# A fixed order for the first weight blocks, two small banks for the first values, and a last norm factor formed earlier

## The chip, the cores and the metric

The kernel runs on one NeuronCore of a Trainium2 chip. TensorE (PE in the profile; PEld are its weight loads) multiplies, VectorE (DVE), ScalarE (ACT) and GpSimd (POOL) work on rows, and SyncE (SP) issues nearly all transfers. The metric is the device time of one execution in microseconds (us), lower is better; a kernel is judged by the median of its runs. A profiled execution is a run of its own: its span is the time between the first and the last record on the core, and its own time is a little longer than that.

## The reference, cut to what matters

Two layers work on 256 positions of 2048 features. Layer 0 mixes with HGRN2, a gated recurrence with 16 heads; layer 1 mixes with a gated MLP. Each layer then has a squared-ReLU MLP, and a last norm closes the trunk.

```python
def rms_norm(x, gain):
    y = xf * lax.rsqrt(jnp.mean(xf * xf, axis=-1, keepdims=True) + NORM_EPS)
    return (y * gain.astype(jnp.float32)).astype(x.dtype)

def hgrn2_mixer(h, w_in, w_out, g_norm, lb):
    proj = h @ w_in                                   # (256, 2048) @ (2048, 8192)
    q, f, i, g = jnp.split(proj, [FORGET_DIM, 2 * FORGET_DIM, 2 * FORGET_DIM + D_MODEL], axis=-1)
    q = jax.nn.silu(q)
    forget = lb + (1.0 - lb) * jax.nn.sigmoid(f)
    k = 1.0 - forget
    log_f = jnp.log(forget)
    v = i
    ...                                               # decayed scores of q and k, times v, chunk by chunk
    return o @ w_out

for i in range(DEPTH):
    hn = rms_norm(h, norm_mix[i])
    h = h + mixer(hn)
    h = h + sq_relu_mlp(rms_norm(h, norm_mlp[i]), mlp_w1[i], mlp_w2[i])
return rms_norm(h, final_norm)
```

## The kernel before, in words

All large products are done in two parts. ACT casts each block of weights to a rounded high part (line 128), DVE subtracts that from the block and leaves the low part (line 129), and PE forms high x high and low, then low x high, in PSUM (lines 159 and 161 where features come out on partitions, 170 to 172 where positions do). The activations `S1` hold a high and a low half in the same way. Each weight tile (`wt`) holds 1024 numbers of 128 rows in both parts; there are five such buffers, and three raw buffers (`raw`) that SP loads ahead.

HGRN works on pairs of heads, `hp` from 0 to 7. The weight blocks are used in the order forget gate, query, values, output gate; the values of two pairs are formed together (every even `hp`), 512 columns wide, by `mm_wide` in `pw2`. For the first pair the forget block (`pw0`, `pw_149` in the order of instructions) and the query block (`pw1`, `pw_150`) are special: x arrives in four chunks of 512 features, and for each chunk `to_features` transposes it on PE (line 196), scales it by the norm's gain into the high and low half of `S1` (line 200 on ACT, 201 on DVE), and both weight blocks are multiplied for the chunk. The squares of x (lines 260 and 263) are summed beside that, and only when all are there is the norm's factor `r0c` formed: a mean on DVE (lines 265 to 268), a power on POOL (line 269), a spread over all partitions by two matmuls on PE (`pb_a`, line 276), a copy into `R0`. The products of `pw0` and `pw1` are taken out of PSUM (lines 179, 180), multiplied by `R0` (line 182), and a long chain on ACT and DVE follows (lines 326 to 413): exponentials, logarithms, a running sum `c` (line 340), differences `dl` and decayed factors `gl`. From these PE forms the scores (`sc` line 420, `sd` line 428, `st` line 435, `sx` line 440), which DVE copies under masks into `Px` and `Pm`.

PSUM is split into two pools: two wide tiles of two banks each (`psw`, tag `pw`) and four single banks (`pss`, which hands out a bank for every transpose, score and spread by `bank(name)`). `pw2`, the first values, takes a wide tile, and so waits until `pw0` has been taken out.

Which instruction stands where in each engine's queue is decided while the program is built, by a scheduler with a timeline of its own; the code's order and `tc.high_priority` are only hints to it. Every engine then runs its queue in the order that it was given.

At the end the last 512 columns are done in two blocks of 256, for 128 positions at a time. `last_rows` adds the product to the stream, squares it with a running sum on ACT (line 644), and multiplies it by the last gain on DVE (line 645); `finish` forms the row factor (lines 669 to 671), scales four pieces of 512 columns on DVE and ACT in turn (lines 675, 677) and sends them out (line 678).

Of the kernel before, what the change touches and what calls it, by code (L numbers as in the profile page):

```python
# [8 lines left out]
F32 = mybir.dt.float32  # L9
# [6 lines left out]
P = 128  # L16
# [17 lines left out]
def trunk(ctx: ExitStack, tc: tile.TileContext, x, norm_mix, norm_mlp, final_norm, hgrn_w_in, hgrn_w_out,  # L34
# [83 lines left out]

    def split_weights(n, raw, q, parts=1):
# [3 lines left out]
        wt = pool.tile([P, 2048], FR, tag=tag, name=f"wt{n}_{q}").rearrange("p (k n) -> p k n", k=kw)  # L123
        src = raw[:, kw * (q % 2):kw * (q % 2) + kw, :]
        with tc.high_priority(offset=PRIO if n > 1 else 0):
            for i in range(parts):
# [3 lines left out]
        ready.setdefault(n, []).append(wt)  # L130

# [24 lines left out]
    def mm_feat(pt, wts, xs, ks=range(KT), run=8):  # L156
        for tiles in runs(wts, xs, ks, run):
            for wt, xk, k, n in tiles:
                M.matmul(pt[:, n, :], lhsT=wt[:, n * P:(n + 1) * P], rhs=xk, start=(k == 0), stop=False)  # L159
            for wt, xk, k, n in tiles:  # L160
                M.matmul(pt[:, n, 256:512], lhsT=wt[:, 256 + n * P:256 + (n + 1) * P], rhs=xk[:, 0:256],  # L161
                         start=False, stop=(k == KT - 1))

    def mm_wide(pt, wts, xs):
        for k in range(KT):
            wt = wts[k // 2][:, k % 2, :]
            xk = xs[k // 2][:, k % 2, :]
            for n in range(2):
                hi, lo = xk[:, n * P:(n + 1) * P], xk[:, 256 + n * P:256 + (n + 1) * P]
                M.matmul(pt[:, n, :], lhsT=hi, rhs=wt[:, 0:512], start=(k == 0), stop=False)  # L170
                M.matmul(pt[:, n, :], lhsT=hi, rhs=wt[:, 512:1024], start=False, stop=False)  # L171
                M.matmul(pt[:, n, :], lhsT=lo, rhs=wt[:, 0:512], start=False, stop=(k == KT - 1))  # L172

# [14 lines left out]

    def to_features(c, gains):

        for i in (2 * c, 2 * c + 1):
            pt = bank(f"xT{i}")
            for k in range(2):
                o = (2 * i + k) * P
                for j in range(2):
                    M.transpose(pt[:, k * T + j * P:k * T + (j + 1) * P], ht[:, j, o:o + P], ident)  # L196
            for k in range(2):
                g = gains[:, 2 * i + k:2 * i + k + 1]
                ptk = pt[:, k * T:(k + 1) * T]
                S.activation(S1[i][:, k, 0:256], ptk, AF.Copy, scale=g)  # L200
                V.scalar_tensor_tensor(S1[i][:, k, 256:512], ptk, g, f32(S1[i][:, k, 0:256]),  # L201
                                       op0=ALU.mult, op1=ALU.subtract)
# [7 lines left out]
    cols = cp.tile([P, 81], F32, name="cols")  # L210
    if WARM:
        wps = bank("wps")
        for i in range(WARM):
            M.matmul(wps[:, 0:P], lhsT=ones, rhs=ones, start=True, stop=True)
    warm = cp.tile([P, 1], F32, name="warm")
    S.activation(warm, epsc, AF.Exp)
# [4 lines left out]
    with tc.tile_pool(name="x0", bufs=1) as x0, tc.tile_pool(name="x1", bufs=2) as x1:  # L221
# [15 lines left out]
        pw = [psw.tile([P, 2, 512], F32, tag="pw", name=f"pw{n}") for n in range(2)]  # L237
        pc = bank("pc0")
        M.transpose(pc[:, 0:32], rows0, ident[0:32, 0:32])
        V.tensor_copy(cols0, pc[:, 0:32])  # L240
# [14 lines left out]
        V.tensor_copy(cols, pc[:, 0:81])  # L255
        for c in range(4):
            for j in range(2):
                junk = x1.tile([P, 512], F32, tag="junk", name=f"junk{c}{j}")
                if j:
                    V.scalar_tensor_tensor(junk, xt[c][:, j, :], 1.0, xt[c][:, j, :], op0=ALU.mult, op1=ALU.mult,  # L260
                                           accum_out=ssp[:, j, c:c + 1])
                else:
                    S.activation(junk, xt[c][:, j, :], AF.Square, accum_out=ssp[:, j, c:c + 1])
        s2 = x0.tile([P, 2, 2], F32, name="s2")
# [34 lines left out]
    with tc.tile_pool(name="hg", bufs=1) as hg, tc.tile_pool(name="hg2", bufs=2) as hg2:  # L299
# [14 lines left out]
        for hp in range(NP):  # L314
# [129 lines left out]
            if hp % 2 == 0:  # L444
                wts, pt = take()
                mm_wide(pt, wts, S1)
                vv = hg.tile([P, 2, 512], F32, tag="v", name=f"v{hp}")
                for j in range(2):
                    with tc.high_priority(offset=PRIO_EV):
                        S.activation(vv[:, j, :], pt[:, j, :], AF.Copy, scale=r0c[:, j:j + 1])  # L450
            v = vv[:, :, hp % 2 * 256:hp % 2 * 256 + 256]
# [189 lines left out]

    def normed(hs, c0, width, i, j):
        jk = fin2.tile([P, 512], F32, tag="jk", name=f"jk{i}{j}")
        S.activation(jk[:, 0:width], hs, AF.Square, accum_out=ssf[:, j, i:i + 1])
        V.tensor_tensor(hs, hs, fnb[:, c0:c0 + width], op=ALU.mult)

# [7 lines left out]
    def last_rows(pj, wts, i, j):  # L654
# [10 lines left out]
        V.scalar_tensor_tensor(hs, pj, r2c[:, j:j + 1], hs, op0=ALU.mult, op1=ALU.add)  # L665
        normed(hs, c0, 256, i, j)

    def finish(j):
        V.tensor_tensor(mf[:, j:j + 1], ssf[:, j, 4:5], pre[:, j:j + 1], op=ALU.add)
        V.tensor_scalar(mf[:, j:j + 1], mf[:, j:j + 1], 1.0 / D, EPS, op0=ALU.mult, op1=ALU.add)  # L670
        G.tensor_tensor(rf[:, j:j + 1], mf[:, j:j + 1], mhalf[:, 0:1], op=ALU.pow)
        for c, w in enumerate((512, 512, 512, 512)):
            hs = ht[:, j, c * 512:(c + 1) * 512]
# [4 lines left out]
            (nc.sync, nc.scalar)[c % 2].dma_start(out=out[0, j * P:(j + 1) * P, c * 512:(c + 1) * 512], in_=hs)  # L678

# [8 lines left out]
    for i in (3, 4):  # L688
        wts, pt = take()
        if i == 4:  # L690
            s2 = fin.tile([P, 2, 2], F32, name="s2")
            V.tensor_tensor(s2, ssf[:, :, 0:2], ssf[:, :, 2:4], op=ALU.add)
            V.tensor_tensor(pre, s2[:, :, 0], s2[:, :, 1], op=ALU.add)
        for j in range(2):
# [42 lines left out]
```

## Time and profile before

| what | value |
|---|---|
| median of 3 runs | 2202.48 us (2202.46 to 2202.97) |
| profiled execution, its own time | 2203.23 us |
| its span | 2201.4 us |
| PE busy | 2186.8 us, 99% |
| PE weight loads | 1882.0 us, 85% |
| DVE busy | 1342.9 us, 61% |
| ACT busy | 1049.3 us, 48% |
| bytes read from HBM | 410.44 MB, 187 GB/s over the span |

Busy time is the union of an engine's records. PE is in use nearly all the time, so what the time can lose or gain lies in stretches in which PE has nothing to do, and in the clock that PE is granted.

### The profile page before, as it was taken

The numbers are of one execution on the slowest core, as the hardware profiler recorded it, in microseconds if no ns is written. First come the engines' busy times: TensorE is split into PE (matmuls) and PEld (weight loads), VectorE is DVE, ScalarE is ACT, GpSimd is POOL, SyncE is SP. The second block draws the span as 40 slices with busy tenths as digits, with TensorE's granted clock in tenths as the row PEclk, the third lists the DMA queues.
The fourth block names the chain that finished last, engine by engine and source line by source line (L and its number), as shares of the span: only waits on it lengthen the run. The fifth ranks groups of instructions, "written<-read, shape, count | busy, mean of one in ns | idle before, by whom it ended". The sixth has DMA issues, their size and how long they took to land.

```text
span 2201.4 us, 27791 instructions
## 1 busy us (share of the span) xinstructions
PE 2186.8 (99%) x11400; PEld 1882.0 (85%) x11400; DVE 1342.9 (61%) x1657; ACT 1049.3 (48%) x1293; POOL 10.8 (0%) x25
## 2 busy tenths in 40 slices
PE   8999999999999999999999999999999999999998
PEld 7888888888888888888888888888888888888887
DVE  7787887766645555555555567656555645554554
ACT  6666665655434434434444544444434433443443
POOL 1000000000000000000000000000000000000000
PEclk9999999999999999999999999999999999999999
DMA  7555555556655565665666556656566556556653
GB/s 239 171 176 169 173 172 163 192 178 188 205 192 178 188 210 178 188 209 179 187 208 206 183 182 205 209 188 194 180 203 191 191 184 198 191 191 191 192 186 121
DMA packets 309889, 414.34 MB, mean 188 GB/s; under 512 B 6801, under 2 KB 210946, under 8 KB 309506
## 3 DMA queue, kind: packets, MB, share of 16 engines
q1 hardware_dynamic: 309138, 411.50, 58.6%
q8 instruction: 89, 1.46, 0.3%
q10 hardware_dynamic: 624, 1.07, 0.1%
q14 instruction: 38, 0.31, 0.0%
HBM read 410.44 MB, written 2.10 MB: 187 GB/s over the span
## 4 chain that ended last, share of the span: by engine, by line
PE 99%; DMA 0%; issue 0%; ACT 0%; SPq 0%; DVE 0%; POOLq 0%; POOL 0%; ACTq 0%
PE pw L159 32%; PE pw L161 17%; PE pw L170 16%; PE pw L172 16%; PE pw L171 16%; PE sc L420 1%; PE xT L196 1%; DMA raw<-in_hgrn_w_in 0%; PE sd L428 0%; PE mix L621 0%; PE po L455 0%; PE pw L662 0%; PE pw L661 0%; PE pw L660 0%; PE pn L464 0%
## 5 line engine op out<-in xcount | busy, mean ns | idle before, releaser
L129 DVE TENSOR_TENSOR wt<-raw,wt 128x1024 fp32r<-128x1024 f32 (+1 forms) x769 | 923.6, 1219 | 741.7 <-ACT wt L128 741.0
L128 ACT CAST wt<-raw 128x1024 fp32r<-128x1024 f32 (+1 forms) x769 | 790.3, 1049 | 895.8 <-PE pw L172 451.0
L159 PE MATMUL pw<-s,wt 128*128 128x512 f32 x3072 | 728.5, 392 | 4.8 <-ACT wt L128 2.7
L159 PEld LDWEIGHTS pw<-s,wt 128*128 128x128 f32 x3072 | 569.3, 189 | 118.4 <-ACT wt L128 3.4
L170 PE MATMUL pw<-wt,s 128*128 128x512 f32 x1504 | 586.6, 390 | 0.0
L172 PE MATMUL pw<-wt,s 128*128 128x512 f32 x1504 | 586.2, 390 | 0.0
L171 PE MATMUL pw<-wt,s 128*128 128x512 f32 x1504 | 586.0, 390 | 0.0
L161 PEld LDWEIGHTS pw<-s,wt 128*128 128x128 f32 x3072 | 388.3, 191 | 10.7
L161 PE MATMUL pw<-s,wt 128*128 128x256 f32 x3072 | 396.0, 283 | 0.0
L172 PEld LDWEIGHTS pw<-wt,s 128*128 128x128 f32 x1504 | 282.3, 188 | 58.3
L170 PEld LDWEIGHTS pw<-wt,s 128*128 128x128 f32 x1504 | 282.4, 188 | 57.9 <-DVE z_f L180 0.2
L171 PEld LDWEIGHTS pw<-wt,s 128*128 128x128 f32 x1504 | 282.4, 188 | 57.6
L186 ACT CAST s<-a 128x512 fp32r<-128x512 f32 x64 | 39.7, 620 | 135.6 <-DVE a L540 135.6
L187 DVE TENSOR_TENSOR s<-a,s 128x512 fp32r<-128x512 f32 x64 | 44.3, 692 | 37.1 <-ACT s L186 37.1
L540 DVE SCALAR_TENSOR_TENSOR a<-z_ff 128x512 f32<-128x512 f32 x64 | 43.8, 684 | 0.3
L180 DVE TENSOR_TENSOR z_ff<-pw,tb_ff 128x512 f32<-128x512 f32 x64 | 43.7, 682 | 0.0
L179 ACT COPY tb_ff<-pw 128x512 f32<-128x512 f32 x64 | 37.3, 582 | 0.0
L200 ACT ACTIVATE s<-xT,cols 128x256 fp32r<-128x256 f32 x64 | 27.9, 473 | 17.6 <-PE xT L196 11.2
L201 DVE SCALAR_TENSOR_TENSOR s<-xT,cols,s 128x256 fp32r<-128x256 f32 x64 | 28.6, 478 | 8.2 <-ACT s L200 8.0
L519 DVE SCALAR_TENSOR_TENSOR ht<-pw,col_c,ht 128x512 f32<-128x512 f32 x32 | 22.5, 745 | 5.3 <-PE pw L172 5.3
L519 DVE SCALAR_TENSOR_TENSOR ht<-pw,col_e,ht 128x512 f32<-128x512 f32 x30 | 21.1, 746 | 4.6 <-PE pw L172 4.6
L196 PE MATMUL xT<-ident,ht 128*128 128x128 f32 x128 | 19.3, 282 | 0.6 <-DMA ht<-in_x 0.6
(196 smaller groups left out, 724.0 us busy)
## 6 DMA issues: line engine op xcount, KB each, us to landing
raw<-in_mlp_w SPq DMA_DIRECT2D x256, 1024.0 KB, 5.7
raw<-in_hgrn_w_in SPq DMA_DIRECT2D x60, 1024.0 KB, 5.8
raw<-in_gmlp_w_in SPq DMA_DIRECT2D x32, 1024.0 KB, 5.5
raw<-in_hgrn_w_out SPq DMA_DIRECT2D x16, 1024.0 KB, 5.1
raw<-in_gmlp_w_out SPq DMA_DIRECT2D x16, 1024.0 KB, 5.2
raw<-in_hgrn_w_in SPq DMA_DIRECT2D x7, 512.0 KB, 9.5
ht<-in_x SPq DMA_DIRECT2D x3, 512.0 KB, 9.2
gb<-in_gmlp_ln_gain SPq DMA_DIRECT2D x8, 128.0 KB, 5.2
```

The costliest lines, as they stand in the source:

```text
L128: S.copy(wt[:, kk, 0:width], src[:, kk, :])
L129: V.tensor_tensor(wt[:, kk, width:2 * width], src[:, kk, :], f32(wt[:, kk, 0:width]), op=ALU.subtract)
L159: M.matmul(pt[:, n, :], lhsT=wt[:, n * P:(n + 1) * P], rhs=xk, start=(k == 0), stop=False)
L161: M.matmul(pt[:, n, 256:512], lhsT=wt[:, 256 + n * P:256 + (n + 1) * P], rhs=xk[:, 0:256], start=False, stop=(k == KT - 1))
L170: M.matmul(pt[:, n, :], lhsT=hi, rhs=wt[:, 0:512], start=(k == 0), stop=False)
L171: M.matmul(pt[:, n, :], lhsT=hi, rhs=wt[:, 512:1024], start=False, stop=False)
L172: M.matmul(pt[:, n, :], lhsT=lo, rhs=wt[:, 0:512], start=False, stop=(k == KT - 1))
L180: V.tensor_tensor(dst, pt[:, :, 0:256], tb, op=ALU.add)
L187: V.tensor_tensor(dst[:, :, 256:512], src, f32(dst[:, :, 0:256]), op=ALU.subtract)
L196: M.transpose(pt[:, k * T + j * P:k * T + (j + 1) * P], ht[:, j, o:o + P], ident)
L519: V.scalar_tensor_tensor(hs, pt[:, j, :], 1.0 if col is None else col[:, j:j + 1], hs, op0=ALU.mult, op1=ALU.add)
L540: V.scalar_tensor_tensor(a.rearrange("p a t -> p (a t)"), z.rearrange("p a t -> p (a t)"), 0.0, z.rearrange("p a t -> p (a t)"), op0=ALU.m ...
```

## The change

Four things are changed.

1. The first weight blocks: the code of the start is cut into steps, and `step` ties each step's instructions behind those of the step before on each engine, so that the scheduler can't change their order. Within a step it may. The steps multiply `pw0` by halves and quarters of a chunk, and the squares of x stand between (`squares`). Three more small matmuls on ones (`keep_warm(3)`) stand before the first product.
2. In `to_features` the two copies of ACT now stand ahead of the two of DVE (everywhere).
3. The values of the first pair (`hp == 0`) are summed in two single banks (`take(single=True)`) and no longer in a wide tile.
4. The last norm factor is formed as soon as the last square is summed, ahead of the multiplication by the gain, in one DVE instruction in place of two; the four pieces that are scaled and sent are 640, 384, 640 and 384 columns wide.

```diff
+    last = {}
+    def step(make):
+        traced = nc.cur_bb.bb.instructions
+        with ExitStack() as behind:
+            for ins in last.values():
+                behind.enter_context(tc.issue_after(ins))
+            n = len(traced)
+            make()
+        for ins in traced[n:]:
+            last[ins.engine] = ins
...
-    def take():
+    def take(single=False):
...
+        if single:
+            return ready.pop(n), [bank(f"pw{n}_{j}") for j in range(2)]
         return ready.pop(n), psw.tile([P, 2, 512], F32, tag="pw", name=f"pw{n}")
...
             for k in range(2):
                 ...
                 S.activation(S1[i][:, k, 0:256], ptk, AF.Copy, scale=g)
+            for k in range(2):
+                ...
                 V.scalar_tensor_tensor(S1[i][:, k, 256:512], ptk, g, f32(S1[i][:, k, 0:256]),
                                        op0=ALU.mult, op1=ALU.subtract)
...
-        for c in range(4):
-            to_features(c, cols0)
-            for n in range(2):
-                split_weights(n, raws[n][c // 2], c, parts=1 if c or n else 2)
-                mm_feat(pw[n], ready[n], S1, range(4 * c, 4 * c + 4))
+        step(gains0)
+        step(lambda: split_weights(0, raws[0][0], 0, parts=2, only=0))
+        step(lambda: to_features(0, cols0, (0,)))
+        step(lambda: split_weights(0, raws[0][0], 0, parts=2, only=1))
+        step(lambda: to_features(0, cols0, (1,)))
+        step(lambda: keep_warm(3))
+        step(lambda: multiply(0, 0, 2))
+        step(lambda: multiply(0, 2, 4))
+        step(lambda: split_weights(1, raws[1][0], 0))
+        for c in range(4):
+            step(lambda: multiply(1, 4 * c, 4 * c + 2))
+            if c < 3:
+                step(lambda: to_features(c + 1, cols0))
+                step(lambda: split_weights(0, raws[0][(c + 1) // 2], c + 1))
+            step(lambda: squares(c))
+            step(lambda: multiply(1, 4 * c + 2, 4 * c + 4))
+            if c < 3:
+                step(lambda: multiply(0, 4 * c + 4, 4 * c + 8))
+                step(lambda: split_weights(1, raws[1][(c + 1) // 2], c + 1))
...
-                wts, pt = take()
+                wts, pt = take(hp == 0)
                 mm_wide(pt, wts, S1)
...
-        normed(hs, c0, 256, i, j)
+        normed(hs, c0, 256, i, j, (lambda: factor(j)) if i == 4 else None)
+    def factor(j):
+        V.tensor_scalar(mf[:, j:j + 1], ssf[:, j, 4:5], pre[:, j:j + 1], 1.0 / D, op0=ALU.add, op1=ALU.mult)
+        G.tensor_tensor(rf[:, j:j + 1], mf[:, j:j + 1], mhalf[:, 0:1], op=ALU.pow)
```

What the scheduler makes of it stands in the order of instructions. The first place is PE's queue from the end of the first two blocks (`pw_149` forget, `pw_150` query) to the first values and scores. Before (`pw_613` are the values, `sc_0` and `sc_1` the first two scores):

```order
L159 MATMUL pw_150<-s_7_96,wt_3_361 128x512 x2
L161 MATMUL pw_150<-s_6_95,wt_3_361 128x256 x4
L161 MATMUL pw_150<-s_7_96,wt_3_361 128x256 x4
L170 MATMUL pw_613<-wt_0_450,s_0_89 128x512
L171 MATMUL pw_613<-wt_0_450,s_0_89 128x512
...
L170 MATMUL pw_613<-wt_7_477,s_7_96 128x512
L171 MATMUL pw_613<-wt_7_477,s_7_96 128x512
L420 MATMUL sc_0_566<-gl_32_522 128x128 x2
L420 MATMUL sc_1_570<-gl_16_530 128x128 x2
L172 MATMUL pw_613<-wt_7_477,s_7_96 128x512
```

In the change, PE's queue at the same place (the values are now `pw_0_616` and `pw_1_617`):

```order
L178 MATMUL pw_150<-s_7_96,wt_3_376 128x512 x4
L180 MATMUL pw_150<-s_7_96,wt_3_376 128x256 x4
L324 MATMUL pb_a<-dg_a_484,ones 128x128
L324 MATMUL pb_a<-dg_a_487,ones 128x128
L468 MATMUL sc_0_569<-gl_32_525 128x128 x2
L468 MATMUL sc_1_573<-gl_16_533 128x128 x2
L468 MATMUL sc_2_577<-gl_8_541 128x128 x2
L468 MATMUL sc_4_581<-g_0_559 128x128 x2
L476 MATMUL sd_585<-qd_547,kd_548 128x128 x4
L483 MATMUL st_592<-ident,Px_445 128x128 x2
L488 MATMUL sx_596<-gx_563 128x128 x2
L192 MATMUL pw_0_616<-wt_0_453,s_0_89 128x512
```

The spread of the norm's factor and all the scores of the first pair now stand ahead of the first product of the values, where before the values began right behind the query block and the spread stood inside it.

The second place is DVE's queue at the end of the start. Before, the mean of the squares (lines 265 to 268) stood ahead of the low part of the fourth forget tile (`wt_3_342`):

```order
L260 SCALAR_TENSOR_TENSOR junk_403,ssp<-ht 128x512
L201 SCALAR_TENSOR_TENSOR s_4_93<-xT_268,cols_109,s_4_93 128x256
L265 TENSOR_TENSOR s_405<-ssp 128x4
L201 SCALAR_TENSOR_TENSOR s_5_94<-xT_277,cols_109,s_5_94 128x256
L267 TENSOR_TENSOR ms<-s_405 128x2
L268 TENSOR_SCALAR ms<-ms 128x2
L129 TENSOR_TENSOR wt_3_342<-raw_1_132,wt_3_342 128x4x256
```

In the change the mean (`s_408`, then `ms`) stands here (`wt_0_453` to `wt_4_469` are the tiles of the values):

```order
L146 TENSOR_TENSOR wt_0_453<-raw_0_451,wt_0_453 128x2x512
L146 TENSOR_TENSOR wt_1_456<-raw_0_451,wt_1_456 128x2x512
L333 TENSOR_TENSOR lbw<-cols,lbw 128x16 x3
L146 TENSOR_TENSOR wt_2_461<-raw_1_459,wt_2_461 128x2x512
L313 TENSOR_TENSOR s_408<-ssp 128x4
L202 TENSOR_TENSOR z_f_492<-pw_149,tb_f_491 128x512
L146 TENSOR_TENSOR wt_3_464<-raw_1_459,wt_3_464 128x2x512
L202 TENSOR_TENSOR z_q_513<-pw_150,tb_q_512 128x512
L315 TENSOR_TENSOR ms<-s_408 128x2
L146 TENSOR_TENSOR wt_4_469<-raw_2_467,wt_4_469 128x2x512
L335 TENSOR_TENSOR lbw<-lbw 128x16
L316 TENSOR_SCALAR ms<-ms 128x2
```

The mean moved behind the low parts of all eight tiles of the first two blocks and of five tiles of the values, and behind both sums that take the products out.

## Rows read from the trace of the kernel before

**Rows 1.** The page, part 4: the chain that ended last, by engine.

```profile
PE 99%; DMA 0%; issue 0%; ACT 0%; SPq 0%; DVE 0%; POOLq 0%; POOL 0%; ACTq 0%
```

**Rows 2.** Waits of PE, whole span: us, times, longest (first and last of four).

```profile
PE pw L159 <- ACT wt L128: 2.7, 1, 2.7
...
PE xT L196 <- DMA ht<-in_x: 0.6, 1, 0.6
```

**Rows 3.** Windows: length, busy (x) of PE, PEld, DVE, ACT, POOL; PEclk, DMA, GB/s.

```profile
8.00:12.36 4.36, 1.22 (x2) 0.50 (x2) 0.83 (x4) 1.13 (x3) 0.00 (x0) 0.50 1.03 335
12.36:16.00 3.64, 3.64 (x13) 3.15 (x14) 3.25 (x7) 2.45 (x7) 0.00 (x0) 0.50 1.07 369
17.00:18.00 1.00, 1.00 (x4) 0.76 (x4) 1.00 (x2) 1.00 (x3) 0.00 (x0) 0.61 1.05 384
```

**Rows 4.** Timeline of the start: start us, us, engine, line, operation [idle before].

```profile
11.27 1.04 ACT L128 CAST wt<-raw 128x1024 fp32r<-128x1024 f32 x1 [3.23 <-DMA raw<-in_hgrn_w_in]
12.36 1.22 PE L159 MATMUL pw<-s,wt 128*128 128x512 f32 x2 [2.67 <-ACT wt L128]
26.18 0.83 ACT L200 ACTIVATE s<-xT,cols 128x256 fp32r<-128x256 f32 x2
34.44 2.35 DVE L129 TENSOR_TENSOR wt<-raw,wt 128x1024 fp32r<-128x1024 f32 x2
```

**Rows 5.** Timeline around the first values and the first scores, PEld and PE.

```profile
40.24 0.19 PEld L170 LDWEIGHTS pw<-wt,s 128*128 128x128 f32 x1 [0.20 <-DVE z_f L180]
...
59.87 1.05 PE L420 MATMUL sc<-gl 128*128 128x128 f32 x8
```

**Rows 6.** The chain in order of time, 0 to 80 us: start us, us, what.

```profile
27.64 0.44 PE xT L196 x4
33.29 0.94 PE pw L161 x8
34.23 2.75 PE pw L159 x12
...
60.03 0.89 PE sc L420 x8
68.31 0.89 PE sd L428 x8
```

**Rows 7.** Groups by line and form, 40.2 to 72 us: xcount | busy, mean ns.

```profile
L372 ACT ACTIVATE dl<-dl 128x512 f32<-128x512 f32 x3 | 1.9, 633 | 2.6 <-DVE dl L371 2.4
L422 DVE COPY_PREDICATED Px<-masks,sc 128x256 f32<-128x256 uint8 x4 | 1.8, 441 | 0.1
L378 DVE TENSOR_TENSOR gl<-dl,q 128x128 f32<-128x128 f32 x6 | 1.5, 283 | 0.0
L334 ACT ACT_TABLE_LOAD x1 | 1.3, 1283 | 0.0
L370 DVE TENSOR_TENSOR dl<-c 128x256 f32<-128x256 f32 x3 | 1.2, 417 | 0.0
L340 DVE TENSOR_TENSOR_SCAN c<-reset,l 128x512 f32<-128x512 f32 x1 | 1.2, 1217 | 0.0
L382 DVE TENSOR_TENSOR dl_d<-c 128x512 f32<-128x512 f32 x1 | 0.7, 683 | 0.0
```

**Rows 8.** Groups of POOL, whole span: the same columns.

```profile
L269 POOL TENSOR_TENSOR r0c<-ms,mhalf 128x2 f32<-128x2 f32 x1 | 1.8, 1800 | 24.8 <-DVE ms L268 24.8
...
L511 POOL TENSOR_TENSOR col_c<-m_c,mone 128x2 f32<-128x2 f32 x1 | 0.7, 701 | 475.6 <-DVE m_c L506 475.6
```

**Rows 9.** Timeline of the last 8 us, DVE, POOL and ACT.

```profile
2194.42 0.42 DVE L645 TENSOR_TENSOR ht<-ht,fnb 128x256 f32<-128x256 f32 x1 [0.58 <-ACT jk L644]
2194.76 0.15 DVE L669 TENSOR_TENSOR mf<-ssf,pre 128x1 f32<-128x1 f32 x1
...
2195.18 0.55 POOL L671 TENSOR_TENSOR rf<-mf,mhalf 128x1 f32<-128x1 f32 x1 [4.91 <-DVE mf L670]
2195.77 1.33 ACT L675 ACTIVATE ht<-ht,rf 128x512 f32<-128x512 f32 x2 [1.38 <-POOL rf L671]
```

More of the change, by code (lines that the diff above doesn't have):

```diff
@@ L117, in raw_tile, with split_weights @@
         return raw.rearrange("p (k n) -> p k n", n=specs[n][3])
-    def split_weights(n, raw, q, parts=1):
+    last = {}
[8 more added lines that the diff above has]
+            last[ins.engine] = ins
+    def split_weights(n, raw, q, parts=1, only=None):
         width = specs[n][3]
@@ L122, in split_weights @@
         pool, tag = (more["wt"], "wx") if "wt" in more and q == 3 and n < more["end"] else (wtp, "wt")
-        wt = pool.tile([P, 2048], FR, tag=tag, name=f"wt{n}_{q}").rearrange("p (k n) -> p k n", k=kw)
+        if not only:
+            wt = pool.tile([P, 2048], FR, tag=tag, name=f"wt{n}_{q}").rearrange("p (k n) -> p k n", k=kw)
+            ready.setdefault(n, []).append(wt)
+        else:
+            wt = ready[n][-1]
         src = raw[:, kw * (q % 2):kw * (q % 2) + kw, :]
         with tc.high_priority(offset=PRIO if n > 1 else 0):
-            for i in range(parts):
+            for i in range(parts) if only is None else (only,):
                 kk = slice(i * kw // parts, (i + 1) * kw // parts)
@@ L162, in mm_feat, with part @@
                          start=False, stop=(k == KT - 1))
+    def part(pt, j):
+        return pt[j] if isinstance(pt, list) else pt[:, j, :]
     def mm_wide(pt, wts, xs):
@@ L187, in split, with to_features @@
         V.tensor_tensor(dst[:, :, 256:512], src, f32(dst[:, :, 0:256]), op=ALU.subtract)
-    def to_features(c, gains):
-        for i in (2 * c, 2 * c + 1):
+    def to_features(c, gains, halves=(0, 1)):
+        for i in (2 * c + h for h in halves):
             pt = bank(f"xT{i}")
@@ L200, in to_features @@
                 S.activation(S1[i][:, k, 0:256], ptk, AF.Copy, scale=g)
+            for k in range(2):
+                g = gains[:, 2 * i + k:2 * i + k + 1]
+                ptk = pt[:, k * T:(k + 1) * T]
                 V.scalar_tensor_tensor(S1[i][:, k, 256:512], ptk, g, f32(S1[i][:, k, 0:256]),
@@ L210, in trunk, with keep_warm @@
     cols = cp.tile([P, 81], F32, name="cols")
-    if WARM:
-        wps = bank("wps")
-        for i in range(WARM):
+    wps = bank("wps")
+    def keep_warm(n):
+        for i in range(n):
             M.matmul(wps[:, 0:P], lhsT=ones, rhs=ones, start=True, stop=True)
+    keep_warm(WARM)
     warm = cp.tile([P, 1], F32, name="warm")
@@ L237, in trunk, with gains0, squares, multiply @@
         pw = [psw.tile([P, 2, 512], F32, tag="pw", name=f"pw{n}") for n in range(2)]
-        pc = bank("pc0")
-        M.transpose(pc[:, 0:32], rows0, ident[0:32, 0:32])
-        V.tensor_copy(cols0, pc[:, 0:32])
-        for c in range(4):
-            to_features(c, cols0)
-            for n in range(2):
-                split_weights(n, raws[n][c // 2], c, parts=1 if c or n else 2)
-                mm_feat(pw[n], ready[n], S1, range(4 * c, 4 * c + 4))
+        def gains0():
+            pc = bank("pc0")
+            M.transpose(pc[:, 0:32], rows0, ident[0:32, 0:32])
+            V.tensor_copy(cols0, pc[:, 0:32])
+        def squares(c):
+            for j in range(2):
+                junk = x1.tile([P, 512], F32, tag="junk", name=f"junk{c}{j}")
+                if j:
+                    V.scalar_tensor_tensor(junk, xt[c][:, j, :], 1.0, xt[c][:, j, :], op0=ALU.mult, op1=ALU.mult,
+                                           accum_out=ssp[:, j, c:c + 1])
+                else:
+                    S.activation(junk, xt[c][:, j, :], AF.Square, accum_out=ssp[:, j, c:c + 1])
+        def multiply(n, k0, k1):
+            mm_feat(pw[n], ready[n], S1, range(k0, k1))
+        step(gains0)
[7 more added lines that the diff above has]
+        step(lambda: split_weights(1, raws[1][0], 0))
+        for c in range(4):
+            step(lambda: multiply(1, 4 * c, 4 * c + 2))
[7 more added lines that the diff above has]
+                step(lambda: split_weights(1, raws[1][(c + 1) // 2], c + 1))
         state["load"] = state["use"] = 2
@@ L255, in trunk @@
         V.tensor_copy(cols, pc[:, 0:81])
-        for c in range(4):
[L257 to L263, printed above, removed]
         s2 = x0.tile([P, 2, 2], F32, name="s2")
@@ L693, in trunk @@
             V.tensor_tensor(pre, s2[:, :, 0], s2[:, :, 1], op=ALU.add)
+            V.tensor_scalar(pre, pre, EPS * D, None, op0=ALU.add)
         for j in range(2):
```

22 lines of the change are left out of this document (10 added, 12 removed).

## The prediction

> **What bounds the kernel now.** I read the page's chain first: PE is on it for 99% [rows 1]. The waits of PE come next: four in the whole span, the longest 2.7 us, the shortest 0.6, and all of them in the first 13 us [rows 2]. From the cast that starts at 11.27 us, when the first query block lands, and the product behind it at 12.36 [rows 4], PE has an unbroken stream of work. So there is little to win (the first 12 us, the last 8, and the clock), and anything that makes PE wait later is paid in full, since no other engine holds PE's work back anywhere else and nothing could be caught up. In windows the granted clock shows 0.50, PE's lower level of 1.2 GHz, from 8 to 16 us, first with PE nearly idle and then with it busy, and it comes back between 17 and 18 us [rows 3].
>
> The place that matters is 40.24 us. There the first values begin right behind the query block; their first weight load waited 0.2 us for the sum that empties `pw0` [rows 5]. The first scores come 19.6 us later, at 59.87, in the middle of PE's products for the values [rows 5]. In between ACT and DVE work through the long chain from `R0` to the scores, and PE covers all of it with the products of the values.
>
> **The change, part by part.** The order of instructions takes this cover away: the spread `pb_a` and every score now stand ahead of the first product of the values. PE takes its products in queue order, as far as the trace shows: `sc_0` and `sc_1` ran between the last products of the values, where the order of before has them. So the values wait for the whole chain. Weight tiles are prepared meanwhile, but five buffers hold five of the eight.
>
> The Trainium skill, PSUM — Partial Sum Buffer, section Engine vs sequencer instructions, says that matmuls start and complete in program order and only weight loads may be pulled ahead. The trace agrees at the place just named.
>
> I add up when the values can begin, first with PE at full clock. A DVE or ACT instruction holds its engine some 0.09 us less than its row says (two low parts in 2.35 us are 1.13 apart; two copies in 0.83 are 0.40 apart [rows 4]).
>
> *Start.* The first query cast begins at 11.27 as before, since the same load ends its wait. Behind it come four products (0.9), its low part at 13.6 and four small ones (0.5), so the transposes of the second chunk begin at 14.1. A chunk costs PE eight transposes (2 x 0.44), 16 wide products (16 x 0.229 = 3.7) and 16 narrow ones (16 x 0.118 = 1.9) [rows 6], and a wait of about 0.8: the forget products need four copies and a cast behind the first transposes (0.5 + 4 x 0.40 + 1.05 = 3.1), against 2.3 of work in PE's queue. That makes 7.2 a chunk. Transposes of the fourth chunk then begin at 28.5, and the query block ends at 28.5 + 3.1 + 2 x 2.8 = 37.2, 3.0 earlier than the 40.24 of before. That is the gain of the fixed order.
>
> *To the mean.* The fourth query cast ends near 33, and from 33.6 DVE has no pause: six low parts (6 x 1.13), two sums (2 x 0.60), a square (0.76), about eight small ones (8 x 0.17) make 10.1, so the mean is there at 43.7.
>
> *To `R0` and the running sum.* The power took 1.8 us on POOL where the same work elsewhere took 0.7 [rows 8]; I take 1.8, the row of this very instruction, which gives 45.5. Two diagonals, the spread (0.45), the copy and the multiplication by `R0` make 2.2: 47.7. ACT then does exponential and tanh (2 x 0.54), a table load, two logarithms of 256 columns (0.8, as the two copies in [rows 4]), one of 512 (0.54), a second table load and a tanh (0.63), with 1.28 for each load: 5.6, so 53.3. The query's product (0.6) and the scan (1.22) give 55.1 [rows 7].
>
> *To the last score.* DVE's 31 instructions from the first `dl` to the last copy into `Px` have no low parts of weights between them any more: four of 512 columns at 0.60, fourteen of 256 (four of them masked copies) at 0.33 to 0.36, eleven of 128 at 0.20, two of 64 at 0.12, 9.6 in sum [rows 7], and some 0.5 for handovers: 10.1. That is 65.2, and `st` and `sx` put the first values at 66.3.
>
> Of this, the scores are work that before came later: four `sc` (8 passes for two of them, 0.89, so 1.8), `sd` 0.9 [rows 6], `st` and `sx` 0.7, together 3.4. Net at full clock: 66.3 - 40.24 - 3.4 = +22.7. It can't be won back, since PE is the bound behind it.
>
> *The clock.* PE idles from about 38 to 66 but for short bursts. Between 8 and 12.36 it was busy for 1.22 of 4.36 us, at 0.50 [rows 3], so I take the lower level for the stall. The spread, `sc_4`, `sd`, `st` and `sx` lie on the chain and take twice as long: +2.5. The values then begin at the lower level; before, PE worked from 12.36 to past 17 until the level rose, which costs half of nearly 5 us: +2.4 (lower bound 0, if the scores have brought the clock back). In the first chunk I expect the dip as well, because PE, by the same sums done with the forget block's first products near 10.4, still waits until 12.4 for the query block; doubling the first products and transposes gives +1.7. Together 6.6; bounds 0 and 9 (the last if the clock comes back twice as late).
>
> The Trainium skill, TensorE: Matmul & The Clock Gate, section What's actually happening, says that the throttled state is the default and activity releases it, and gives half rate for it. The 0.50 in the trace agrees; by that rule alone the whole stall is at 1.2 GHz.
>
> *The rest.* The three more warming matmuls lie in a wait (PE was busy for 1.22 of the 4.36 us before 12.36 [rows 3]). The two copies ahead of the two subtractions in `to_features` cost nothing: PE never waits for them outside the start, and if that cover were gone each `to_features` could shift by one 0.4 us copy. Weights behind the stall: PE frees the first tile 23 products into the values, wants the sixth at product 60, 8.5 us later, and a cast and a low part take 2.4; no second wait.
>
> *The end.* The factor passes the multiplication by the gain (0.34 between starts) and loses one of the two small instructions that stand between 2194.76 and the power's start at 2195.18 (about 0.2) [rows 9]: -0.53. ACT's two pieces shrink from 512 to 384 columns: by columns 1.33 becomes 1.07, -0.27; DVE's two of 640 end at about the same time. Together -0.8, bounds -0.4 and -1.0. The power and the gain now run side by side.
>
> Sum: 22.7 + 6.6 - 0.8 = 28.5. The profiled execution of before would go from 2203.2 to 2231.7; against the median of 2202.5, 2231.
>
> **The rivals.**
>
> *A: the clock doesn't fall* (or returns at once). For it: short bursts of PE stand through the stall. Against it: 0.50 at 8 to 12 us with such bursts. Time: 2202.5 + 22.7 - 0.8 = 2224.4.
>
> *B: a second wait behind the stall.* Only five tiles are ready, and the load of the third raw buffer after that starts only when the sixth tile is split, about 8 us into the values. For it: prefetch has been at a standstill for 20 us. Against it: PE has 22 us of value products, and 1 MB at the table's 187 GB/s is 5.6 us. If one load is late by its length: 2231 + 5.6 = 2236.6.
>
> *C, the other side: the chip doesn't hold the values back.* If the values' products could start while the scores wait, cover is as before, and only the gains stand: 3.0 at the start (less 1.7 if the clock dips) and 0.8 at the end, so 2198.7 to 2200.4. It decides where the first product of the values starts: near 38 us or past 60. Against it stands the order itself, and that before ran as its order says.
>
> *D: the stall is far shorter than I add*, since weights no longer break the chain. To end within 0.2% it would have to cost under 8 us net of the start's 3.0 and the end's 0.8; the two table loads, the power and DVE's last 31 instructions alone are 14.5. Time: 2203 plus or minus 4.
>
> **How the numbers follow.** Forecast (stall at the lower clock) 0.70, A 0.16, B 0.07, C 0.05, D 0.02. The time is that of the forecast, 2231. Its own bounds: 22.7 is worked out from some sixty rows with an error of 2 to 3; the clock's 6.6 can be 3 to 9. That makes 2225 to 2236, which takes in A but for its lower half, and B. I give 2223 to 2237; C lies outside. A measurement of this kernel can tell about 0.2% (4.4 us) from no change. Faster by more than that: C reaches at best 3.8 us, so only part of it, 0.03; within: the rest of C and D, 0.04; slower: 0.93.
>
> **What would show it.** Right: the scores run before the first values; PE has no work but `pb_a` and bursts of scores between about 38 and 68 us; its longest wait names DVE on a score; the granted clock reads 0.50 for a stretch there; `pw1` ends at 37 to 39. POOL's power starts past 40 us. At the end the factor's POOL row starts some 0.5 us after the last square. Wrong: values starting near 40 us, or a second wait of PE after 70 us, or a clock that stays at 1.00.

## The result, and the profile of the changed kernel

The changed kernel takes 2226.08 us (median of 4 runs, 2225.40 to 2227.87); the kernel before, measured beside it, took 2202.47. The ratio is 1.0112, with a 95% interval of 1.0100 to 1.0124: slower by 1.0 to 1.2%, inside the range given, and 23.6 us where 28.5 were added up. The profiled execution, the slowest of the four, has a span of 2226.1 us, 24.7 more than that of before.

The page of the changed kernel, busy time, and the chain by engine, as in [rows 1]:

```profile
PE 2191.4 (98%) x11406; PEld 1886.3 (85%) x11406; DVE 1343.0 (60%) x1656; ACT 1047.8 (47%) x1293; POOL 11.0 (0%) x25
...
PE 66%; issue 32%; DVE 1%; ACT 1%; DMA 0%; SPq 0%; POOL 0%; POOLq 0%; ACTq 0%
```

The shares by engine say little here. The waits of PE say it at once; [rows 2] had none above 2.7 us:

```profile
PE sc L468 <- DVE gl L426: 12.9, 2, 11.9
PE pb_a L324 <- DVE dg_a L323: 7.1, 1, 7.1
PE pw L178 <- ACT wt L145: 2.5, 4, 0.8
PE sc L468 <- issue: 1.6, 1, 1.6
```

The first and second are the stall: 7.1 us for the diagonals of the spread, then 12.9 for two of the scores. Its stretch in PE's timeline, answering to [rows 5] (start, length, operation, idle time before):

```profile
36.70 0.64 PE L180 MATMUL pw<-s,wt 128*128 128x256 f32 x4
...
44.42 1.20 PE L324 MATMUL pb_a<-dg_a,ones 128*128 128x128 f32 x4 [7.09 <-DVE dg_a L323]
...
57.47 2.26 PE L468 MATMUL sc<-gl 128*128 128x128 f32 x8 [11.85 <-DVE gl L426]
60.79 1.22 PE L468 MATMUL sc<-gl 128*128 128x128 f32 x4 [1.05 <-DVE gl L426]
63.64 1.20 PE L468 MATMUL sc<-g 128*128 128x128 f32 x4 [1.63 <-issue]
64.62 1.92 PE L476 MATMUL sd<-qd,kd 128*128 128x128 f32 x8
66.33 0.64 PE L483 MATMUL st<-ident,Px 128*128 128x128 f32 x2
66.76 1.06 PE L488 MATMUL sx<-gx 128*128 128x128 f32 x4
67.47 0.78 PE L192 MATMUL pw<-wt,s 128*128 128x512 f32 x1
```

The query block ends at 37.34, and the first value, which stood at 40.24 in [rows 5], starts at 67.47, behind every score. The windows of this stretch (length, busy time and count of each engine, granted clock last but two), as in [rows 3]:

```profile
8.00:12.36 4.36, 4.03 (x22) 3.06 (x20) 2.51 (x4) 1.92 (x4) 0.00 (x0) 1.00 1.02 343
12.36:38.00 25.64, 22.71 (x135) 19.38 (x133) 18.38 (x37) 17.21 (x32) 1.75 (x1) 1.00 0.75 260
38.00:45.00 7.00, 0.58 (x3) 0.61 (x4) 6.66 (x16) 1.43 (x3) 2.04 (x4) 0.81 0.88 267
45.00:66.00 21.00, 6.46 (x26) 5.50 (x26) 14.87 (x40) 10.36 (x16) 1.31 (x5) 0.50 0.04 12
66.00:69.50 3.50, 3.50 (x14) 3.11 (x14) 1.51 (x3) 0.37 (x1) 0.00 (x0) 0.50 0.00 0
69.50:72.00 2.50, 2.50 (x12) 2.04 (x11) 0.00 (x0) 0.00 (x0) 0.00 (x0) 0.97 0.00 0
```

Two things are to be seen. The lower level (0.50, 1.2 GHz) stands through the stall, as forecast. But it does not stand at 8 to 12.36 us, where [rows 3] had it: PE is busy there for 4.03 of 4.36 us, and the clock stays at full rate until the stall. Behind the stall it is back at 69.5 us, when PE has worked without a pause since the score at 63.64.

The mean, the power and the end, as in [rows 8, 9] (timeline of DVE, POOL and ACT):

```profile
42.59 0.16 DVE L316 TENSOR_SCALAR ms<-ms 128x2 f32<-128x2 f32 x1
...
42.91 0.71 POOL L317 TENSOR_TENSOR r0c<-ms,mhalf 128x2 f32<-128x2 f32 x1 [17.07 <-DVE lbw L336]
...
2219.05 0.19 ACT L692 ACTIVATION_READ_ACCUMULATOR jk<-ht 128x1 f32 x1
2219.27 0.21 DVE L719 TENSOR_SCALAR mf<-ssf,pre 128x1 f32<-128x1 f32 x1 [0.58 <-ACT jk L692]
...
2220.26 1.12 ACT L726 ACTIVATE ht<-ht,rf 128x384 f32<-128x384 f32 x2 [1.02 <-POOL rf L720]
2220.26 1.01 DVE L728 TENSOR_SCALAR ht<-ht,rf 128x640 f32<-128x640 f32 x2 [0.45 <-POOL rf L720]
```

### The profile page after: what moved, and what is told of

It is laid out like the page before. It is cut to its first block, busy times and chain, and to the rows that moved or that the text cites. A ratio compares the mean times of both kernels' runs of the same rounds, so it can differ in the third digit from the quotient of the medians.

```text
span 2226.1 us, 27833 instructions
## 1 busy us (share of the span) xinstructions
PE 2191.4 (98%) x11406; PEld 1886.3 (85%) x11406; DVE 1343.0 (60%) x1656; ACT 1047.8 (47%) x1293; POOL 11.0 (0%) x25
## 4 chain that ended last, share of the span: by engine, by line
PE 66%; issue 32%; DVE 1%; ACT 1%; DMA 0%; SPq 0%; POOL 0%; POOLq 0%; ACTq 0%
PE pw L178 21%; PE pw L180 11%; PE pw L192 10%; PE pw L194 10%; PE pw L193 10%; PE sc L468 1%; PE xT L218 1%; PE sd L476 0%; DMA raw<-in_hgrn_w_in 0%; PE mix L669 0%; PE po L503 0%; DVE wt L146 0%; PE sx L488 0%; PE pn L512 0%; PE po L504 0%
## 5 line engine op out<-in xcount | busy, mean ns | idle before, releaser
L588 DVE SCALAR_TENSOR_TENSOR a<-z_ff 128x512 f32<-128x512 f32 x64 | 43.7, 684 | 0.3
L202 DVE TENSOR_TENSOR z_ff<-pw,tb_ff 128x512 f32<-128x512 f32 x64 | 43.7, 682 | 0.0
L201 ACT COPY tb_ff<-pw 128x512 f32<-128x512 f32 x64 | 37.2, 581 | 0.0
L468 PE MATMUL sc<-gl 128*128 128x128 f32 x96 | 15.6, 297 | 12.9 <-DVE gl L426 12.9
L468 PEld LDWEIGHTS sc<-gl 128*128 128x128 f32 x96 | 14.2, 208 | 14.3 <-issue 12.1
L567 DVE SCALAR_TENSOR_TENSOR ht<-pw,col_c,ht 128x512 f32<-128x512 f32 x32 | 22.5, 746 | 5.4 <-PE pw L194 5.4
```

Of the source, the lines that this page charges most:

```text
L202: V.tensor_tensor(dst, pt[:, :, 0:256], tb, op=ALU.add)
L468: M.matmul(sc[:, b * P:(b + 1) * P], lhsT=gl[:, 0, b * P:(b + 1) * P], rhs=gl[:, 1, b * P:(b + 1) * P], start=True, stop=True)
L588: V.scalar_tensor_tensor(a.rearrange("p a t -> p (a t)"), z.rearrange("p a t -> p (a t)"), 0.0, z.rearrange("p a t -> p (a t)"), op0=ALU.m ...
```

## The experiments

The theory: the small banks put the values behind the scores in PE's queue, and the stall is the length of the chain from the mean to the scores. The main rival: the fixed start order does it, since it brings the mean 16 us later. Three groups ran together, each on one chip beside the kernel before: e1 to e4 (median of before 2201.81), e5 to e8 (2201.35), e9 and e10 (2201.13).

| run | median us | ratio to before | 95% interval | first value | span |
|---|---|---|---|---|---|
| e1 wide tile | 2203.62 | 1.0008 | 1.0000 to 1.0017 | 38.89 | 2200.3 |
| e2 banks alone | 2221.04 | 1.0087 | 1.0074 to 1.0101 | 59.99 | 2218.6 |
| e3 banks asked for early | 2227.23 | 1.0114 | 1.0099 to 1.0130 | 67.44 | 2225.8 |
| e4 end alone | 2201.81 | 1.0001 | 0.9992 to 1.0010 | 38.45 | 2200.2 |
| e5 banks written early | 2200.50 | 0.9995 | 0.9986 to 1.0004 | 36.65 | 2200.0 |
| e6 e5 and early mean | 2200.56 | 0.9997 | 0.9988 to 1.0005 | 36.16 | 2199.9 |
| e7 early mean alone | 2225.51 | 1.0109 | 1.0095 to 1.0123 | 65.64 | 2224.4 |
| e8 clock held | 2225.46 | 1.0108 | 1.0094 to 1.0122 | 65.24 | 2222.8 |
| e9 e6, even pieces | 2200.68 | 0.9997 | 0.9989 to 1.0006 | 34.47 | 2198.0 |
| e10 old start, banks early | 2201.73 | 1.0002 | 0.9993 to 1.0011 | 38.78 | 2199.9 |

First value and span are those of the one profiled execution. The start of one execution differs from another's by 1 to 2 us: the query block of the old start ends at 40.24, 38.45, 38.22 and 38.95 us in the kernel before, e4, e2 and e10. What differs ahead of that is the load of the first query weights, on which ACT's cast waits (the cast starts at 11.27, 10.41, 9.71 and 10.02), and the granted clock behind it: from 16 to 17 us it is still 0.50 in the kernel before and 1.00 in the other three.

**e1: the wide tile again.** The changed kernel with

```
-                wts, pt = take(hp == 0)
+                wts, pt = take()
```

> The changed kernel with one edit undone: the first values take the wide tile again; fixed start order and the new end stay. Theory (the small banks make the values stand behind the scores on PE): the stall is gone, the values begin at 37.3 us right behind the query block, and the start's 2.9 us and some 0.2 us of the end remain as a gain: 2202.5 - 3.1 = 2199.4; up to 2202 if the first scores, whose chain now also begins later, make PE wait for them. Rival (the fixed start order costs the time, because it makes the mean of squares 16 us later: power on POOL at 42.9 us and not at 26.3): the loss stays for the most part, 2218 or more.

The stall is gone and with it 22.5 us, as the theory has it. Its number, 2199.4 to 2202, was missed: of the start's gain nothing is left. PE's longest wait in e1, and the first value:

```profile
PE pw L192 <- DVE z_f L202: 2.4, 1, 2.4
```

```profile
35.88 0.64 PE L180 MATMUL pw<-s,wt 128*128 128x256 f32 x4
38.89 0.50 PE L192 MATMUL pw<-wt,s 128*128 128x512 f32 x1 [2.37 <-DVE z_f L202]
```

The query block ends at 36.52, but the wide tile has to wait until the sum on DVE has emptied `pw0`, which costs 2.4 us here and 0.2 in [rows 5]. The small banks take this wait away; they need no tile of the other pool.

**e2: the small banks alone.** The kernel before with `take(single)`, `part` and the two banks of the change, nothing else.

> The kernel before with one edit: the first values are summed in two small banks. Start order and end are those of before. Theory: the stall comes from this edit alone. Its length is that of the chain from the multiplication by R0: 67.6 - 46.06 = 21.5 us in the changed kernel, and here it starts at 40.22, so the values begin near 62 in place of 40.24, with 3.4 us of score work done before them: about +18.5, and about 1 for a clock that is at its lower level at first: 2222 (2218 to 2225), a little less than the changed kernel, because the mean is early here. Rival (start order costs the time): 2202 to 2203.

2221.04, in the theory's range (2218 to 2225). The edit alone makes the stall. It is shorter than the changed kernel's, since the old order has the mean early: the values begin 21.8 us after the query block's end (38.22 to 59.99), against 30.1 (37.34 to 67.47) in the changed kernel. So under the small banks the fixed order costs 8.4 us of stall. In the traces the first value comes 7.5 us later with it; the medians, of two groups, are 5.0 us apart (the changed kernel's trace is the slowest of its four executions, e2's the second fastest of its four).

**e3 and e5: what holds the values back.** e3 asks for the two banks ahead of the spread; e5 also writes two products of ones into them there (the values' first product overwrites these).

```
             else:
+                early = [bank(f"pw2_{j}") for j in range(2)]
+                for b in early:                                    # e5 only
+                    M.matmul(b[:, 0:P], lhsT=ones, rhs=ones, start=True, stop=True)
                 pt = pw[0]
                 prefetch()
                 spread(R0, r0c, "a")
...
-                wts, pt = take(hp == 0)
+                wts, pt = take(early if hp == 0 else None)
```

> The changed kernel, still with two small banks, but they are asked for before the spread and the scores, and not behind them. Theory (banks are handed out in the order in which the program asks for them, and four at a time): the values stand ahead of the scores again and begin at 37.3 us; as with the wide tile 2199.4, up to 2202. Two banks are left for xT, spread and scores meanwhile; they aren't short of them, since PE has the values to do. Rival (sums in two small banks are slow in themselves, or the clock falls for another reason): 2215 or more.

> The changed kernel, still with two small banks. They are asked for ahead of the spread, as in e3, and two tiny products write into them there; the first product of the values (start=True) overwrites that. Theory, as e3 left it: a bank is handed out where the program first writes into it, in the order of these first writes, so that asking early did nothing and writing early is enough. Then the values follow the query block at once, near 36.6 us, without e1's wait of 2.4 us for the sum that empties pw0; PE has no wait past 14 us: 2199 to 2202, the best case about 2.4 below e1. Rival (sums in two small banks are slow in themselves): 2215 or more.

e3 did not do what it was made for: its order of instructions still has all scores ahead of the values, and its trace is that of the changed kernel. The theory's words on it ("in the order in which the program asks for them") are refuted. In e5 the values stand ahead of the spread, and the stall is gone, still with small banks: so sums in two small banks are not slow in themselves, and what moved the values ahead was the early write into the banks, not the early request. All waits of PE in e5, and its first values:

```profile
PE pw L178 <- ACT wt L145: 2.6, 3, 1.6
PE wps L240 <- POOL mhalf L59: 1.1, 1, 1.1
```

```profile
36.65 0.62 PE L192 MATMUL pw<-wt,s 128*128 128x512 f32 x2
37.10 0.64 PE L180 MATMUL pw<-s,wt 128*128 128x256 f32 x4
```

No wait is left past the start, e1's 2.4 us are gone too, and the values begin between the query block's last products. Even so the kernel is only 0.05% below the kernel before, and the interval holds 1.

**e4: the end alone**, the kernel before with `factor`, `normed`, `finish` and `pre` of the change.

> The kernel before with the new end alone: the last factor formed ahead of the multiplication by the gain, pieces of 640 and 384 columns. By the prediction's term -0.8: 2201.7. By the trace of the changed kernel, where the scale started 1.02 us after the square and not 1.38, but the span ended 6.86 us and not 7.0 after it: -0.15: 2202.3.

No difference that can be measured (0.9992 to 1.0010). In its trace the scale starts 1.02 us after the square, as in the changed kernel, but from the end of the square's sum to the end of the span e4 needs 7.60 us, where the kernel before needs 7.01 and the changed one 6.86. This trace stands apart: the seven others with the new end need 6.79 to 6.88. With the old end, the kernel before and e10 need 7.01 and 6.99, and e2 7.84. Only e2 and e4 move an instruction load (queue q14) in the last 7 us, and in both the transfers of SP's queue land late (3.0 us for 256 KB and 3.4 for 320, where the others of their sizes have 2.5 and 3.0). Without these two the new end is some 0.17 us shorter.

**e6 and e7: an earlier mean**, in e5 and in the changed kernel:

```
-            step(lambda: squares(c))
+            for s in (((0, 1), (2,), (3,), ())[c]):
+                step(lambda: squares(s))
```

> As e5, and each square is taken one step of the start earlier. Theory: the mean comes some 4 us sooner, but the products of the values hide the chain behind it, so nothing changes: as e5, 2199 to 2202. Rival (the first scores are awaited in e5, because the spread stands behind 60 of the values' products): 2 to 4 us faster than e5.

> The changed kernel with one edit: each square is taken one step of the start earlier, so that the sums behind the last squares come sooner on DVE. The values still stand behind the scores. Theory (in the stall everything hangs on the mean, one for one): the power starts 3.5 to 4.5 us earlier than 42.91, the values as much earlier than 67.6, and the time is 2222 (2221 to 2223.5). Rival (the stall hangs on the weights or on the logarithms' tables and not on the mean): 2226.

In e6 nothing changes: the products of the values hide the chain again, but for a wait of 0.3 us on one score. In e7's trace the power starts at 38.85, 4.1 us earlier, but the diagonals only 1.5 earlier (DVE, from the mean to the diagonals):

```profile
38.53 0.17 DVE L317 TENSOR_SCALAR ms<-ms 128x2 f32<-128x2 f32 x1
38.60 0.69 DVE L202 TENSOR_TENSOR z_f<-pw,tb_f 128x512 f32<-128x512 f32 x1
39.20 1.22 DVE L146 TENSOR_TENSOR wt<-raw,wt 128x1024 fp32r<-128x1024 f32 x1
40.33 0.69 DVE L202 TENSOR_TENSOR z_q<-pw,tb_q 128x512 f32<-128x512 f32 x1
40.93 1.22 DVE L146 TENSOR_TENSOR wt<-raw,wt 128x1024 fp32r<-128x1024 f32 x1
...
42.15 0.48 DVE L324 TENSOR_SCALAR dg_a<-ident,r0c 128x128 f32<-128x128 f32 x2
```

Four long instructions stand between them on DVE, two of them low parts of weights. The spread starts 1.84 earlier (42.58), the values 1.83 (65.64), and the span is 1.7 shorter: one for one from the spread on. But the expectation was missed. Of the 4.1 us by which the power comes earlier, DVE's queue takes more than half back ahead of the spread, so the stall hangs on what stands in that queue, weights among it, as well as on the mean. The median, 2225.51, is the rival's number and not the theory's 2222; against the changed kernel's 2226.08, of another group, it can't tell 1.7.

**e8: the clock held** by products of ones in the spread's and the scores' banks:

```
+    def hold(pt, n, after):
+        with tc.issue_after(after):
+            for i in range(n):
+                M.matmul(pt[:, 0:P], lhsT=ones, rhs=ones, start=True, stop=True)
```

> The changed kernel with 98 products of ones by ones (128x128) on PE inside the stall: 28 ahead of the spread, 52 ahead of the first score, 10 and 8 ahead of two later ones, each group short enough to end before the data comes. They change no result. Theory (part of the loss is the clock at its lower level in the stall): the granted clock stays at 1.00; the spread, the last score, sd, st and sx on the chain take half as long (0.6 + 0.5 + 0.9 + 0.5) and the first values run at full rate (about 1): 2226.1 - 3.5 = 2222.6. The prediction's term of 6.6 would give 2219.5. Rival (the clock of the stall costs nothing): 2226, or more where the added products delay a score.

The windows of e8, for the changed kernel's 0.81 and 0.50:

```profile
38.00:45.00 7.00, 6.25 (x56) 6.05 (x55) 6.24 (x16) 0.59 (x3) 3.25 (x7) 1.00 0.87 284
45.00:66.00 21.00, 19.31 (x163) 18.47 (x162) 15.79 (x41) 10.36 (x16) 0.09 (x2) 1.00 0.00 1
```

The clock stays at 1.00. From the spread's start to the first value it takes 22.13 us (43.11 to 65.24), against 23.05 in the changed kernel (44.42 to 67.47), and the 96 products of the values 21.65 (65.24 to 86.89) against 22.67 (67.47 to 90.14). So holding the clock gave back 0.9 + 1.0 = 1.9 us. The rest of the 3.3 us by which the span is shorter came ahead of the spread, where this execution is 1.3 us earlier.

The 0.9 is not all that the lower level cost in the bursts, because the added products also changed the order that the scheduler made. In e8 DVE forms `qd` ahead of the third score's factors and waits for ACT there, and PE takes `sd` ahead of the last score:

```profile
58.58 0.69 DVE L445 TENSOR_TENSOR qd<-qd,q 128x512 f32<-128x512 f32 x1 [0.69 <-ACT qd L443]
```

```profile
62.40 1.06 PE L487 MATMUL sd<-qd,kd 128*128 128x128 f32 x8
63.29 0.61 PE L479 MATMUL sc<-g 128*128 128x128 f32 x4
64.59 0.44 PE L494 MATMUL st<-ident,Px 128*128 128x128 f32 x2 [0.69 <-DVE Px L481]
```

From the scan's end (54.52 in the changed kernel, 52.73 in e8) to the last score's start it takes 9.12 and 10.56 us: the other order costs e8 1.4. From the spread's start to the scan's end e8 is 0.5 shorter (9.62 for 10.10), and from the last score's start to the first value 1.9 (1.95 for 3.83). So the lower level in the bursts costs the changed kernel about 2.3 us. This is an estimate from these rows: 0.5 + 1.9, less up to 0.2, because `sd`, 0.89 at full clock, stands in that last stretch in the changed kernel only, while e8 waits 0.69 there. With the 1.0 behind the stall it is about 3.3.

In the medians e8 is 0.6 us below the changed kernel's of another group, nearer to the rival's 2226 than to the theory's 2222.6. That can't tell 1.9 from nothing; the 1.9 and the 3.3 rest on these two traces.

**e9: even pieces at the end**, e6 with `((0, 512), (512, 1024), (1024, 1536), (1536, 2048))`.

> As e6, but the last rows go out in four pieces of 512 columns, as before, and not of 640 and 384. Theory (the end's gain was given back by its larger transfers: the scale starts 1.02 us after the square's sum in place of 1.38, but 320 KB take 3.0 to 3.4 us to land where 256 KB took 2.5): from the last square's sum to the end of the span 6.6 to 6.7 us, where the kernel before has 7.0 and the changed one 6.86; in the median 0.2 to 0.5 faster than e6, which the rounds can't tell. Rival (the landing doesn't hang on the size): 6.9 to 7.2, because ACT's pieces of 512 take 1.33 in place of 1.12.

Transfers on SP's queue in e9, and the changed kernel's (KB of one, median us from issue to landing; ACT's queue has 2.6 for 256 KB in e9 and 2.8 for 192 KB in the changed kernel):

```profile
out<-ht SPq DMA_DIRECT2D x4, 256.0 KB, 2.6
```

```profile
out<-ht SPq DMA_DIRECT2D x4, 320.0 KB, 3.1
```

From the end of the square's sum (2191.34) to the end of the span (2198.0) it is 6.66 us, in the forecast 6.6 to 6.7. By this one trace the factor ahead of the gain is worth 0.35 us (7.01 before), and the uneven pieces give 0.2 of it back (6.79 to 6.88 in the seven traces that have them). No median here can tell it.

**e10: the old start with banks written early**, the kernel before with the edit of e5.

> The kernel before with the small banks, written into early as in e5; its start order and its end stay. It tells what the fixed start order gives where nothing is lost behind it. Theory (the fixed order brings the query block 1 to 2 us forward, and the rest of it is used up by waits for weights): no wait past 14 us, the values follow the query block at once near 38 us, and the time is that of before less the 0.2 us wait at 40.24: 2201 to 2202.5, about 1 us above e5 and e6 in a call of their own. Rival (the fixed order alone is worth 3 us): 3 us above e9, which has it.

2201.73, where e9, measured beside it, has 2200.68. That is what the theory gave. The intervals against the kernel before (0.9993 to 1.0011 and 0.9989 to 1.0006) overlap; drawing again and again from the eleven times of each run puts the difference of the two medians at -0.3 to 2.5 us, so the rival's 3 is outside, but no difference at all is not. None of e5, e6 and e9 is shown to beat the kernel before.

## Why the prediction was right, and where its sum was off

**The mechanism.** The forecast held in each of its signs: the scores run before the first values, PE has nothing but the spread and bursts between 37.3 and 63.6 us, its longest wait names DVE on a score, the granted clock reads 0.50, the query block ends at 37.3 (37.2 forecast), nothing is won back behind it. e2 shows that the small banks alone do it, e1 and e5 that without that order there is no loss. Rival B's second wait is not there (no wait past 67 us), nor C's early values, nor D's short stall. The clock fell, unlike A, but its cost, 1.9 us given back in e8 and about 3.3 by the rows, lies about halfway between A's nothing and my 6.6. The bounds 2225 to 2236 were said to take in A but for its lower half, and B; A's 2224.4 and B's 2236.6 both lie just outside them, and only the range that was given, 2223 to 2237, holds both.

**The stall's steps at full clock** were good to 1 us each. The mean was ready at 42.75 where 43.7 was added up. From the power's end to the end of the product with `R0` it is 3.1 us (43.62 to 46.75), where 2.2 stood in the sum, 0.6 of the difference being the spread at the lower clock. Then came 5.9 to `thf_q` for 5.6, 1.9 for the scan for 1.8, and 10.8 for 10.1 to the last copy into `Px` (54.52 to 65.3). The first value came at 67.47; I had 70.5 with the clock's 2.5 and 1.7 ahead of it.

**Mis-sized: the clock, 6.6 for about 3.3.** The "dip in the first chunk" of 1.7 did not come: the query block's first product started at 11.44 and not 12.4, and PE was busy at 8 to 12.36. That was luck of the execution in part. The load landed earlier, and the cast in front of that product began at 10.33 and not at 11.27. In e5, which has the same start, the cast began at 11.07, PE waited 1.6 us for it until 12.16, and the granted clock was 0.71 from 12.36 to 16 and 0.50 from 16 to 17; in e6 the cast began at 11.22, but PE had other work until 12.2, and the clock stayed at 1.00. The return to full rate cost 1.0 and not 2.4: I had taken the start of the kernel before, where PE came out of a wait, as the pattern; here the scores from 63.64 on had already worked without a pause. In e2 the clock is 0.60 from 58 to 60 us and 1.00 from 60 to 62, so that there it was back when the values began (59.99). The bursts were sized right, 2.5 for the estimated 2.3, though e8 got only 0.9 of it back.

**Mis-sized: the power, 1.8 for 0.7.** I took "the row of this very instruction". It has 1.79 to 1.80 us in the kernel before, e2, e4 and e10, and 0.71 in the changed kernel and the seven others. In the kernel before it starts at 26.30, together with a low part on DVE that lasts to 27.53:

```profile
26.30 1.23 DVE L129 TENSOR_TENSOR wt<-raw,wt 128x1024 fp32r<-128x1024 f32 x1 [0.16 <-ACT wt L128]
```

1.80 less those 1.1 to 1.2 is 0.6 to 0.7, so the power seems to have waited the low part out; in e2, e4 and e10 a low part starts with it too, within 0.01 us. In e7 it ran beside DVE's `z_f` sum (38.60, above), which reads one operand from PSUM, and took 0.71. In e5 it started 0.04 us ahead of a low part: 0.71 for the power and the usual 1.23 for the low part, so that there neither shows a wait.

A longer POOL instruction, the cast of the masks (128x768 numbers), shows such a wait in both orders. It takes 0.81 to 0.82 us in eight traces, and 1.39 to 1.75 in the other four (the changed kernel, e1, e3, e6), where a low part had started ahead of it. In e7, e8 and e9 the cast starts first by 0.01 to 0.07 us, and the low part takes 1.83 to 1.89. The changed kernel, then e7:

```profile
23.93 1.23 DVE L146 TENSOR_TENSOR wt<-raw,wt 128x1024 fp32r<-128x1024 f32 x1
24.09 1.75 POOL L308 CAST masks<-mf 128x768 uint8<-128x768 f32 x1 [22.56 <-DMA mf<-level_masks]
```

```profile
23.97 0.82 POOL L309 CAST masks<-mf 128x768 uint8<-128x768 f32 x1 [22.44 <-DMA mf<-level_masks]
23.98 1.89 DVE L146 TENSOR_TENSOR wt<-raw,wt 128x1024 fp32r<-128x1024 f32 x1
```

The Trainium skill, SBUF — State Buffer, section SBUF: two separate sides, has a rule for this: a DVE instruction with two SBUF inputs and a GpSimd one that reads SBUF share a port pair, the first to start holds it for its whole length, and the other is blocked. The traces agree where the low part comes first (1.79 to 1.80 for the power, 1.39 to 1.75 for the cast) and where the cast comes first (1.83 to 1.89 for the low part); that the low part is blocked where the power comes first, e5 does not show. No run here moved one of these instructions alone.

**Mis-sized: the end, −0.8 for about −0.15.** The scale did start 0.36 us earlier after the square, less than the 0.53 added up, in part since the power itself took 0.66 for 0.55. I had counted ACT's shorter pieces as a gain and not that DVE's 640 columns make the larger transfer, which lands later (3.1 for 2.6 us). e9's one trace separates the two.

**The start's gain, 3.0, has the right end, in part by luck, and the wrong base.** The query block ends at 37.34, as forecast. But with the earlier load the second chunk's transposes began at 13.28 and not at 14.1, and a chunk then took 7.5 us where 7.2 stood in the sum (the next transposes start at 20.76 and 28.27); the two errors met. And the profiled execution of before was a late one: the three other executions of its start order end at 38.2 to 38.95, and those of the fixed order that have no values in between (e1, e3, e7, e8) at 36.1 to 37.5. The gain is nearer 2 us.

In spans it adds up: the first value 27.2 later, less 3.4 of score work already done, 1.0 for the clock behind it, −0.15 at the end: 24.7, which is the difference of the two spans.

## What to carry to other kernels

Before a buffer is moved to another pool to save a short wait, look at what the new pool's requests and first writes are ordered behind: here a wait of 0.2 us (2.4 with the faster start) was exchanged for 30 us without values, since the new banks came behind a chain that the work in them was meant to hide. A late step off the critical path, like the mean here, costs nothing as long as something covers it (e5 and e6) and shows when the cover is gone (8.4 us of stall between e2 and the change, 1.8 of 4.1 us in e7), so price a reordering together with the edit beside it. And a duration taken from one row of one execution needs a look at what ran beside it.

## What was not expected of the hardware

The same POOL power of 128x2 numbers took 1.79 to 1.80 us where a weights' low part on DVE started with it, and 0.71 elsewhere; between a POOL cast and a low part, whichever started second was the longer one, by up to 0.9 and 0.7 us. Behind 30 us of bursts at 0.50 the clock was back 2.0 us after the first value, at a cost of 1.0 us, and in e2 with the first value. 64 KB more in each of one queue's transfers went with a landing 0.5 us later, which gave back about half of what the earlier factor had brought (0.2 of 0.35 us, e9).
